# The second branch's gate as seven half-size block products per pair of tiles, in a hybrid attention and mLSTM layer

## The chip, the cores and the metric
The kernel runs on one core of one Trainium2 chip. The metric is the device time of one execution, in microseconds; the time shown is the median of three runs. All of the layer's large products are done on TensorE (PE) in fp32 quality: each operand x is split into a high part h (rounded to the matmul format) and a low part l = x - h, and a product is three matmuls, h·h, l·h and h·l. A split is one ScalarE (ACT) copy and one VectorE (DVE) subtraction. SyncE (SP) and GpSimd (POOL) issue most of the DMAs.

## The reference
One layer of a decoder on 512 tokens of width 1024: a norm, one combined input projection, two mixers side by side (block-sparse attention and a chunked mLSTM), merged by two sigmoid gates, an output projection, and a SwiGLU FFN.
```
u = rms_norm(h, norm_mix_g)
qa, ka, va, qk_b, vb, ob, ib, fb, ga, gb = jnp.split(u @ w_in, IN_SPLITS, axis=-1)
ya = moba_attention(rope(qa), rope(ka), va)              # 512 wide
hb = mlstm_chunkwise(qb, kb_, vb, i_pre, f_pre)          # 4 heads x 128
hb = hb * lax.rsqrt(jnp.mean(hb * hb, axis=-1, keepdims=True) + NORM_EPS)
yb = jax.nn.sigmoid(ob) * (hb * mlstm_norm_g)
merged = jax.nn.sigmoid(ga) * (ya @ w_proj_a) + jax.nn.sigmoid(gb) * (yb @ w_proj_b)
h = h + merged @ w_out
h = h + swiglu(rms_norm(h, norm_ffn_g))
return rms_norm(h, norm_final_g)
```
The gates ga and gb are 1024 wide each. The change concerns gb, and the order of what stands around it.

## The kernel before, in words
Everything is kept transposed: a result tile has 128 output columns as partitions and the 512 tokens along the free axis. The input projection and the branch projections are cut into 52 units of 128 output columns (`UNITS`), taken in one fixed order: q, k, va, ob, vb, qkb, then the gates ga 0 to 7 (units 28 to 35) and gb 0 to 7 (36 to 43), then p 0 to 7 (44 to 51). A unit's weights are 128x1024 numbers. SP loads them into a `raw` buffer (seven of these), two units at a time (`load_pair`); `split_unit` (line 206) splits them into `wh` and `wl`, two units ahead of their use; `proj` runs 24 matmuls of 128x512 (`mm3`, lines 213 to 215), and `run_g` (line 592) takes the result from PSUM with one DVE multiplication by the norm's factor `rb`. A unit p holds w_proj_a and w_proj_b for 128 columns: 12 matmuls on ya, 12 on yb, then two sigmoids on ACT and three DVE steps that make a tile of the merged vector mT (lines 612 to 614).

Between the units, the mixers' own instructions are interleaved by a loop over steps (`n`): attention for 16 steps, the mLSTM for 8. Its norm runs per head in three parts: `ml_d1` (squares and a copy `nsb` of the numerator), `ml_d2` (the mean, then rsqrt as Ln, Exp and one Newton step, with lines 334 to 336 from a helper) and `ml_e` (the output gate, and the split of yb).

Behind the units comes `ffn()`. The output projection is done as seven block products (W11, W12, S1, S2, S4, S3, W22) on half the tokens and sums of weight blocks, in place of eight; the sums are formed in DRAM, by an SP copy and an accumulating POOL DMA (`wo_copy`, `wo_sum`), at the unit numbers that the table `SUMS` gives. Its operands (`bq`) are sums and differences of the halves of mT, split in turn (`quarters_a`, `quarters_b`, `quarters_lo`). The FFN's gate and up products follow, 22 items of seven products of 12 matmuls 128x256 each; three of them have their weight sums formed in DRAM too (`gs`, `gt24`).

The Tile scheduler sets each engine's order by priorities. The code's order gives them; inside `ffn()`, `plan` and `at` place work by assumed costs (5440 for a product of the output projection) plus the numbers in the table `Q`.

Of the kernel before, what the change touches and what calls it, by code (L numbers as in the profile page):

```python
# [88 lines left out]
Q = {'leadW11': 9908, 'leadW12': 4893, 'leadS1': 11032, 'leadS2': 5165, 'leadS4': 2571, 'leadS3': 5137, 'leadW22': 3430, 'step': -3359, 'hl': 7300, 'addW11': -1192, 'addW12': 2824, 'addS1': 2078, 'addS2': 1620, 'addS4': 7560, 'addS3': 14758, 'addW22': -1247, 'x': 1583, 'g11': 10592, 'g13': 20503, 'g24': 641, 'g12': 5084, 't00': 3558, 't10': -367, 't11': -569, 't01': 1348, 'sq': 641, 'ev': 300, 'qlo': 8915, 'q4': 4375, 'q35': -263, 'q5': -627, 'q26': -426, 'q6': 3684, 'n2': -7624, 'n2b': -1704, 'base': 294, 'mq': -9909, 'mqs': -14706, 'f35': 1, 'ld0': 6835, 'ld1': 20096, 'ld2': 16796, 'lw': 0, 'ho': 1622, 'lo': 2050, 'so': -829, 'nfirst': 5, 'ldS2': 4505, 'ldS4': 20963, 'ldS3': 22228, 'ldW22': 17677, 'mW12': 6692, 'mS2': 12719, 'mS4': 20328, 'mS3': 3928, 'mW22': 16520}  # L89
# [7 lines left out]
def hybrid_layer_kernel(ctx: ExitStack, tc, xT, xtm, wall, wwo, wgu, wds, wdl, g3v, vecs, wgates, consts, rope, out):  # L97
# [90 lines left out]
    wstate = {"pair": 0, "split": 0}  # L188
# [3 lines left out]
    def load_pair():  # L192
        p = wstate["pair"]
        if p * 2 >= NU:
            return
        for u in (2 * p, 2 * p + 1):
            raw[u] = blk(name="raw", raw=True)
            nc.sync.dma_start(raw[u], wall[u])
        wstate["pair"] += 1

    def split_unit():
# [176 lines left out]
    def fill(n=1, mid=None):  # L378

        for _ in range(n):  # L380
# [5 lines left out]
            while wstate["split"] <= min(u + LOOK, NGEN - 1):  # L386
# [195 lines left out]
    gz = {}  # L582

    def run_g(kind):
        def fn(i, wh, wl):
# [7 lines left out]
            gz[(kind, i)] = z  # L593
        return fn
# [7 lines left out]
    def run_p(m, wh, wl):  # L602
        if m % 4 == 0:
            mT.append(slot4(name="mT"))
        pa, pb = mmb(), mmb()
        mm3(pa, wh, wl, range(4), [t[0] for t in ya], [t[1] for t in ya], True, True)
        marks["p", m] = mm3(pb, wh, wl, range(4, 8), [t[0] for t in yb], [t[1] for t in yb], True, True)
        yield
        ga, gb = gz.pop(("ga", m)), gz.pop(("gb", m))
        act_(ga, ga, AF.Sigmoid)  # L610
        act_(gb, gb, AF.Sigmoid)
        V.tensor_tensor(ga, pa, ga, op=ALU.mult)
        V.tensor_tensor(gb, pb, gb, op=ALU.mult)
        V.tensor_tensor(mT[m // 4][:, m % 4, :], ga, gb, op=ALU.add)
# [102 lines left out]
    def wo_sum(k, src):  # L717
        if src == "g":
# [669 lines left out]
    def ffn():  # L1388
# [42 lines left out]
        fill(2)  # L1431
# [283 lines left out]
    def ml_c(h, b, ats):  # L1715
# [3 lines left out]
        for j in ((0, 1), (2, 3))[b]:  # L1719
# [6 lines left out]
            T.matmul(o, vh[:, v], al, start=False, stop=j == 3)  # L1726
# [6 lines left out]
    def ml_d1(h):  # L1733
# [4 lines left out]
        V.tensor_copy(nsb, num)  # L1738
# [3 lines left out]
    def ml_d2(h, sqn, d2, nsb):  # L1742
# [4 lines left out]
        V.scalar_tensor_tensor(d2, d2, EPS * 128.0, ps, op0=ALU.mult, op1=ALU.add)  # L1747

        V.tensor_scalar(d2, d2, 2.0**-39, None, op0=ALU.mult)
# [36 lines left out]
    while n < len(steps) or qa or qb:  # L1786
# [30 lines left out]
        while qb and (qb[0][4] <= n - LC):  # L1817
# [37 lines left out]
def _pack(inp):  # L1855
# [8 lines left out]
    qk = _tiles(w_in[:, np.concatenate(cols)])  # L1864
    parts = {
# [68 lines left out]
```

## Time and profile before
| | |
|---|---|
| median of 3 runs | 727.38 us (727.01 to 727.42) |
| the profiled execution | 727.58 us |
| its span (first to last instruction) | 725.7 us |
| mean granted TensorE clock | 0.997 |
| input products, gates among them, until | 303.0 us of the span |
| projection units p | 303.0 to 346.5 us |
| output projection, FFN, final norm | from 346.5 us |
| moved by DMA | 133.68 MB, 184 GB/s in the mean |

The profile is of one execution. Busy times are shares of the span; the page's chain follows the work that ended last backwards. Row groups give the source line, the engine, the operation, the tile names (written<-read), the shapes, the count, busy time and mean duration, and the idle time ahead with what ended it.

### The profile page before, as it was taken

What the parts mean: (1) busy time and instruction counts of PE and PEld (TensorE: products, weight loads), DVE (VectorE), ACT (ScalarE), POOL (GpSimd) and SP (SyncE); (2) the same over time, 40 slices, a digit from 0 to 9 for tenths busy, and PEclk for the clock granted to TensorE, in tenths of its full rate; (3) what the DMA queues carried; (4) which work ended last, traced back from release to release, by engine and by line L of the source; (5) the groups of instructions that cost most, each with busy time, mean ns of one, the idle gap of its engine ahead of it and who ended that gap; (6) DMA issues with size and microseconds to landing.
All of it is one profiled execution on the core that took longest, in us unless ns stands there. A gap on an engine that the chain in (4) does not pass through costs nothing.

```text
span 725.7 us, 11396 instructions
## 1 busy us (share of the span) xinstructions
PE 715.8 (99%) x4167; PEld 632.4 (87%) x4167; DVE 623.4 (86%) x1090; ACT 441.7 (61%) x778; POOL 78.7 (11%) x100
## 2 busy tenths in 40 slices
PE   8999999999999999999999999999999999999995
PEld 6888888888888888888889998999899899899984
DVE  6898886899986688578898998899899899989997
ACT  7534767679755347633678666565555665655555
POOL 0004010101020001000000001300310310220000
PEclk9999999999999999999999999999999999999998
DMA  9778563856576656644594654975985795696403
GB/s 313 279 219 224 186 210 103 224 225 168 202 177 157 172 146 146 219 145 149 136 293 120 203 161 119 239 208 148 206 256 132 175 275 162 155 249 199 153 0 117
DMA packets 54649, 133.68 MB, mean 184 GB/s; under 512 B 5676, under 2 KB 10420, under 8 KB 54464
## 3 DMA queue, kind: packets, MB, share of 16 engines
q1 hardware_dynamic: 38272, 97.73, 39.1%
q0 software_dynamic: 14880, 32.82, 24.8%
q10 hardware_dynamic: 1440, 2.39, 0.9%
q8 instruction: 33, 0.54, 0.3%
q14 instruction: 24, 0.20, 0.1%
HBM read 116.11 MB, written 29.66 MB: 201 GB/s over the span
## 4 chain that ended last, share of the span: by engine, by line
PE 98%; DMA 1%; ACT 0%; issue 0%; DVE 0%; SPq 0%; DVEq 0%; ACTq 0%
PE mm L213 11%; PE mm L215 11%; PE mm L214 11%; PE mm L904 6%; PE mm L905 6%; PE mm L906 6%; PE s L904 3%; PE s L906 3%; PE s L905 3%; PE mm L1155 3%; PE mm L1156 3%; PE mm L1157 3%; PE acc L1649 2%; PE mm L496 2%; PE mm L497 2%; PE mm L498 2%
## 5 line engine op out<-in xcount | busy, mean ns | idle before, releaser
L160 ACT ACTIVATE wh<-raw 128x1024 fp32r<-128x1024 f32 x50 | 52.8, 1058 | 62.5 <-PE mm L214 59.7
L904 PE MATMUL mm<-bq,w 128*128 128x256 f32 x264 | 75.3, 285 | 0.0
L905 PE MATMUL mm<-bq,w 128*128 128x256 f32 x264 | 75.1, 284 | 0.0
L906 PE MATMUL mm<-bq,w 128*128 128x256 f32 x264 | 74.9, 284 | 0.0
L160 ACT ACTIVATE w<-raw 128x1024 fp32r<-128x1024 f32 (+2 forms) x63 | 58.7, 944 | 23.5 <-PE mm L214 10.0
L173 DVE TENSOR_TENSOR wl<-raw,wh 128x1024 fp32r<-128x1024 f32 x50 | 60.6, 1219 | 7.6 <-ACT wh L160 6.8
L851 DVE TENSOR_TENSOR w<-s,w 128x1024 fp32r<-128x1024 f32 x42 | 51.2, 1218 | 7.1 <-ACT w L160 7.1
L213 PE MATMUL mm<-u,wh 128*128 128x512 f32 x136 | 53.6, 394 | 0.0
L215 PE MATMUL mm<-u,wh 128*128 128x512 f32 x136 | 53.2, 391 | 0.0
L214 PE MATMUL mm<-u,wl 128*128 128x512 f32 x136 | 53.2, 391 | 0.0
L213 PE MATMUL mm<-uh,wh 128*128 128x512 f32 x136 | 53.0, 390 | 0.0
L214 PE MATMUL mm<-uh,wl 128*128 128x512 f32 x136 | 53.0, 390 | 0.0
L215 PE MATMUL mm<-ul,wh 128*128 128x512 f32 x136 | 53.0, 390 | 0.0
L160 ACT ACTIVATE w<-s 128x1024 fp32r<-128x1024 f32 (+1 forms) x46 | 46.6, 1019 | 8.4 <-DVE s L861 4.1
L904 PEld LDWEIGHTS mm<-bq,w 128*128 128x128 f32 x264 | 50.7, 192 | 0.4 <-ACT s L160 0.3
L906 PEld LDWEIGHTS mm<-bq,w 128*128 128x128 f32 x264 | 50.7, 192 | 0.0
L905 PEld LDWEIGHTS mm<-bq,w 128*128 128x128 f32 x264 | 50.7, 192 | 0.0
L904 PE MATMUL s<-bq,w 128*128 128x256 f32 x176 | 50.0, 284 | 0.0
L906 PE MATMUL s<-bq,w 128*128 128x256 f32 x176 | 49.9, 284 | 0.0
L905 PE MATMUL s<-bq,w 128*128 128x256 f32 x176 | 49.9, 284 | 0.0
L777 POOL DMA_DIRECT2D s<-in_wgu_dram x19 | 16.7, 881 | 230.3 <-DVE s L1200 53.1
L160 ACT ACTIVATE s<-mm 128x256 f32<-128x256 f32 x44 | 16.6, 377 | 29.8 <-PE mm L906 29.8
(433 smaller groups left out, 2249.5 us busy)
## 6 DMA issues: line engine op xcount, KB each, us to landing
raw<-in_wall_dram SPq DMA_DIRECT2D x50, 512.0 KB, 4.6
raw<-in_wgu_dram SPq DMA_DIRECT2D x22, 512.0 KB, 5.3
raw<-in_wds_dram SPq DMA_DIRECT2D x20, 512.0 KB, 8.0
s<-in_wgu_dram SPq DMA_DIRECT2D x19, 512.0 KB, 5.5
s<-in_wgu_dram POOLq DMA_DIRECT2D x19, 512.0 KB, 6.1
w<-in_wgu_dram SPq DMA_DIRECT2D x22, 256.0 KB, 6.4
ws<-in_wwo_dram POOLq DMA_DIRECT2D x8, 512.0 KB, 8.2
raw<-ws SPq DMA_DIRECT2D x8, 512.0 KB, 3.6
```

The costliest lines, as they stand in the source:

```text
L160: return A.activation(out_, in_, func, **kw)
L173: V.tensor_tensor(l, src, f(h), op=ALU.subtract)
L213: T.matmul(ps, wh[:, c], rh[j], start=start and j == 0, stop=False)
L214: T.matmul(ps, wl[:, c], rh[j], start=False, stop=False)
L215: i = T.matmul(ps, wh[:, c], rl[j], start=False, stop=stop and j == n - 1)
L851: V.tensor_tensor(dst[1], src, f(dst[0]), op=ALU.subtract)
L904: T.matmul(ps, wh[:, c], bh, start=first and k == 0, stop=False, skip_group_check=not first)
L905: T.matmul(ps, wl[:, c], bh, start=False, stop=False, skip_group_check=not first)
L906: i = T.matmul(ps, wh[:, c], bl, start=False, stop=k == 3, skip_group_check=not first)
L1155: T.matmul(ps, bh, wh[:, d], start=first and k == 0, stop=False, skip_group_check=not first)
L1156: T.matmul(ps, bh, wl[:, d], start=False, stop=False, skip_group_check=not first)
L1157: T.matmul(ps, bl, wh[:, d], start=False, stop=k == 1, skip_group_check=not first)
```

## The change
The eight gb units become four pairs. For a pair of weight tiles, the 1024 weight rows are cut into two halves and the two tiles stand for two blocks of output columns; the token axis is cut into two halves (`A_`, `B_`). This makes a 2x2 by 2x2 block product, done with seven products on half the tokens instead of eight: W11, S2, S1, W12, S3, S4, W22, each 4 x 3 matmuls of 128x256 (`gt_prod`). The weight sums S1 to S4 of a pair are formed in DRAM (`p13`, `p24`) by an SP copy, an accumulating POOL DMA, a second copy and two more accumulating DMAs (`pair_sums`, at the unit numbers in `PS`). The products' token operands are sums of halves of u: x is loaded from DRAM again (`t_load`), scaled by the norm's weight on ACT (`t_scale`), and four operand tiles `top` are formed and split (`t_ops`). The results of a pair are collected by ACT copies and DVE additions (`gt_main`, `gt_last`). One of a pair's two tiles comes out negated, which its sigmoid undoes by a scale of -1.

The units p are divided in pa (two column tiles of w_proj_a per unit) and pb (the same of w_proj_b). PE's order is now ga 0 to 5, pa 0, pa 1, ga 6, ga 7, pa 2, the first pair's W11, pa 3, the rest of the pairs' products (the next pair's W11 stands ahead of a pair's last two products), pb 0 to 3. The sigmoid of ga follows its own product. In the mLSTM's norm, `nsb`'s copy and the Newton step's square move from DVE to ACT and the multiplication by 2^-39 is folded into other instructions; the rsqrt (`ml_d3`) and `ml_e` are called at steps of the pair stage. All values of `Q` are set anew, and the sums for the output projection and `gt24` are formed later.
```
+GATES = [("ga", 6), ("ga", 7)] + [("gb", m) for m in range(8)]
+GPAIRS = [(("gb", 2 * i), ("gb", 2 * i + 1)) for i in range(4)]
...
+PS = {
+    14: [(0, 0), (1, 0)], 17: [(0, 1)], 18: [(1, 1), (2, 0)], 19: [(0, 2)], 20: [(2, 1), (0, 3), (3, 0)], 21: [(1, 2)],
...
+    def t_ops():
+
+        (a, b), (a2, b2) = ((t[:, :, A_], t[:, :, B_]) for t in ux)
+
+        def cut(o, src):
+            t = slot4(F32R, "top").rearrange("p (x k) (e c) -> p x (k e) c", x=2, e=2)
+            top[o] = t
+            act_(t[:, 0], src, AF.Copy)
+            V.tensor_tensor(t[:, 1], src, f(t[:, 0]), op=ALU.subtract)
+
+        V.tensor_tensor(b2, b2, b, op=ALU.subtract)
+        V.tensor_tensor(b, a, b, op=ALU.subtract)
+        cut(1, b)
+        V.scalar_tensor_tensor(a, b2, -1.0, a, op0=ALU.mult, op1=ALU.subtract)
+        cut(4, a)
+        cut(5, b2)
+        V.scalar_tensor_tensor(a2, a, -1.0, a2, op0=ALU.mult, op1=ALU.subtract)
+        cut(6, a2)
...
+    def gt_prep(i):
+
+        g = gtw[i]
+        g["W11"] = split_hl(g["w11"], "w11")
+        for j, (a, b) in enumerate((("S1", "S3"), ("S2", "S4"), ("W22", "W12"))):
+            h, l = split_hl(g[j], dst=(blk2(F32R, "w"), blk2(F32R, "w")))
+            g[a], g[b] = (h[:, 0, :], l[:, 0, :]), (h[:, 1, :], l[:, 1, :])
+            load_pair(1)
+            yield
...
+    def gt_prod(ps, w, o, first=False):
+        wh, wl = w
+        for k in range(4):
+            c = slice(k * P, (k + 1) * P)
+            bh, bl = gt_op(o, k)
+            T.matmul(ps, wh[:, c], bh, start=first and k == 0, stop=False, skip_group_check=not first)
+            T.matmul(ps, wl[:, c], bh, start=False, stop=False, skip_group_check=not first)
+            i = T.matmul(ps, wh[:, c], bl, start=False, stop=k == 3, skip_group_check=not first)
+        marks["unit"] = raw_ins(i)
...
+    def gt_main(i):
+        g = gtw[i]
+        x, s, t, u = g["x"], g["s"], g["t"], g["u"]
+        gt_prod(x, g["S2"], 4)
+        act_(s[:, B_], x, AF.Copy)
         yield
+        z = g["z"] = sb()[:, A_]
+        gt_prod(z, g["S1"], 1, first=True)
+        act_(t[:, B_], z, AF.Copy)
+        yield
+        y = accb()[:, A_]
+        gt_prod(y, g["W12"], 2, first=True)
+        V.tensor_tensor(u[:, A_], y, s[:, A_], op=ALU.add)
+        yield
+        gt_prod(x, g["S3"], 5)
+        V.tensor_tensor(t[:, B_], x, t[:, B_], op=ALU.add)
+        yield
+
+    def gt_last(i):
+        g = gtw.pop(i)
+        x, z, s, t, u = g["x"], g["z"], g["s"], g["t"], g["u"]
+        gt_prod(z, g["S4"], 3)
+        V.tensor_tensor(u[:, B_], z, s[:, B_], op=ALU.add)
+        V.tensor_tensor(t[:, B_], t[:, B_], rb[:, B_], op=ALU.mult)
+        yield
+        gt_prod(x, g["W22"], 6)
+        V.tensor_tensor(t[:, A_], x, rb[:, A_], op=ALU.mult)
+        V.tensor_tensor(u, u, rb, op=ALU.mult)
+        gz[GPAIRS[i][0]], gz[GPAIRS[i][1]] = t, u
+        yield
...
+    def pair_sums(i, j):
+
+        c = lambda x: wgt[i][:, None, S * x : S * x + S].to_broadcast([P, 2, S])
+        if j == 0:
+            nc.sync.dma_start(p13[i], c(0))
+        elif j == 1:
+            nc.gpsimd.dma_start(p13[i], wgt[i][:, 512:1536].rearrange("p (x c) -> p x c", x=2), accum_op=ALU.add)
+        elif j == 2:
+            nc.sync.dma_start(p24[i], p13[i][:, 0:1, :].to_broadcast([P, 2, S]))
+        elif j == 3:
+            nc.gpsimd.dma_start(p24[i], c(2), accum_op=ALU.add)
+        else:
+            nc.gpsimd.dma_start(p24[i][:, 1, :], wgt[i][:, 1536:2048], accum_op=ALU.add)
...
-        V.tensor_copy(nsb, num)
+        act_(nsb, num, AF.Copy)
...
-        V.tensor_scalar(d2, d2, 2.0**-39, None, op0=ALU.mult)
...
-        t = newton(r, d2, lambda: slot(name="nt"))
+        act_(t, r, AF.Square)
+        V.scalar_tensor_tensor(t, t, -(2.0**-40), d2, op0=ALU.mult, op1=ALU.mult)
+        V.scalar_tensor_tensor(t, t, 1.5, r, op0=ALU.add, op1=ALU.mult)
...
+        if n in (24, 25):
+            t_load(n - 24)
+        if n in (24, 26):
+            with behind("unit" if n == 26 else "c"):
+                t_scale(n // 26)
...
+    late = {}
     for h in range(4):
-        if UNITS[pos[0]][0] != "p":
-            fill(1)
-        ml_e(h, norms_out[h])
-    while pos[0] < len(UNITS) and UNITS[pos[0]][0] != "p":
-        fill(1)
+        late.setdefault(Q["d%d" % h], []).append(lambda h=h: ml_t.__setitem__(h, ml_d3(h)))
+    for h in range(4):
+        late.setdefault(Q["e%d" % h], []).append(lambda h=h: ml_e(h))
+    gt_stage(late)
     ffn()
```
Three places of the new order follow; numbers behind names only tell buffers apart, and line numbers are those of each kernel.

DVE, where yb's last head is made ready and the last units begin. Before: `gb` is a gate's evacuation, `wl` the low part of a unit's weights, `yb` that of a head's output.
```order
L1763 SCALAR_TENSOR_TENSOR nt_2913<-nt_2913,vec,ob_2254 128x512
L592 TENSOR_TENSOR gb_3029<-mm_3003,rn_359 128x512
L173 TENSOR_TENSOR yb_3034<-nt_2913,yb_3034 128x512
L173 TENSOR_TENSOR wl_3074<-raw_2924,wh_3073 128x1024
L592 TENSOR_TENSOR gb_3066<-mm_3041,rn_359 128x512
L173 TENSOR_TENSOR wl_3109<-raw_2999,wh_3108 128x1024
```
After: `gg` and `gu` are a pair's two result tiles.
```order
L765 TENSOR_TENSOR gg_3394<-mm_3392,gg_3394 128x256
L772 TENSOR_TENSOR gu_3395<-s_3471,gs_3393 128x256
L187 TENSOR_TENSOR yb_3294<-nt_3143,yb_3294 128x512
L187 TENSOR_TENSOR yb_3356<-nt_3151,yb_3356 128x512
L773 TENSOR_TENSOR gg_3394<-gg_3394,rn_367 128x256
L2001 SCALAR_TENSOR_TENSOR nt_3211<-nt_3211,vec,ob_2276 128x512
L776 TENSOR_TENSOR gg_3394<-mm_3392,rn_367 128x256
L777 TENSOR_TENSOR gu_3395<-gu_3395,rn_367 128x512
L187 TENSOR_TENSOR yb_3356<-nt_3211,yb_3356 128x512
L187 TENSOR_TENSOR wl_3545<-raw_3390,wh_3544 128x1024
L664 TENSOR_TENSOR gg_2977<-mm_3549,gg_2977 128x512
```
Heads 1 and 2 of yb now stand behind pair 3's first evacuations, and the last head behind all of them, next to pb's splits; before, the last head stood ahead of the last two evacuations of gb.

SP, in the loads for the pairs. Before: `gt` is gt24, copied from the sum `gs`.
```order
L198 DMA raw_2999<-in_wall_dram 128x1024
L709 DMA gt_282<-gs_285 256x1x512
L198 DMA raw_3001<-in_wall_dram 128x1024
L198 DMA raw_3077<-in_wall_dram 128x1024
L198 DMA raw_3079<-in_wall_dram 128x1024
```
After: `p` are the sums in DRAM, `in_wgt` the pairs' weights, `in_wall` from the third row off pb's.
```order
L942 DMA gs_293<-in_wgu_dram 256x1x512
L715 DMA raw_3140<-p_286 128x1024
L715 DMA raw_3180<-p_290 128x1024
L939 DMA gt_282<-gs_293 256x1x512
L715 DMA raw_3270<-in_wgt_dram 128x2x512
L1004 DMA w_3920<-in_wgu_dram 128x512
L209 DMA raw_3290<-in_wall_dram 128x1024
L209 DMA raw_3319<-in_wall_dram 128x1024
```
The copy of gt24 stands between pair 3's sums and its W22/W12, ahead of all loads of pb.

PE, at the second product of the output projection. Before: W12 (`acc`, operand `bq_3457`) runs bank by bank.
```order
L914 MATMUL acc_3518<-w_3363,bq_3457 128x512
L915 MATMUL acc_3518<-w_3364,bq_3457 128x512
L916 MATMUL acc_3518<-w_3363,bq_3457 128x512
L914 MATMUL acc_3532<-w_3351,bq_3457 128x512
L915 MATMUL acc_3532<-w_3352,bq_3457 128x512
L916 MATMUL acc_3532<-w_3351,bq_3457 128x512
```
After: `mm` is W11, `s` is S1.
```order
L1149 MATMUL mm_3780<-w_3667,bq_3625 128x512
L1147 MATMUL acc_3806<-w_3671,bq_3745 128x512
L1148 MATMUL acc_3806<-w_3672,bq_3745 128x512
L1147 MATMUL acc_3820<-w_3671,bq_3745 128x512
L1148 MATMUL acc_3820<-w_3672,bq_3745 128x512
L1147 MATMUL s_3872<-w_3687,bq_3629 128x512
L1148 MATMUL s_3872<-w_3688,bq_3629 128x512
L1149 MATMUL s_3872<-w_3687,bq_3629 128x512
```
Two matmuls of W12 for each bank, which read the high part of operand 2 alone, now stand ahead of S1, and the rest of W12 behind it.

More of the change, by code (lines that the diff above doesn't have):

```diff
@@ L187, in hybrid_layer_kernel, with unit_load, load_pair @@
     whl = {}
-    wstate = {"pair": 0, "split": 0}
+    wstate = {"pair": 0, "split": 0, "end": NPLAIN + 2}
     NU = len(UNITS)
     LOOK = 2
[L192 to L199, printed above, removed]
+    gtw = {}
+    def unit_load(u):
+        raw[u] = blk(name="raw", raw=True)
+        nc.sync.dma_start(raw[u], wall[u])
+    jobs = [(unit_load, u) for u in range(2, NPLAIN)]
+    jobs += [(lambda j: gt_load(0, j), j) for j in range(3)]
+    jobs += [(unit_load, u) for u in (NPLAIN, NPLAIN + 1)]
+    jobs += [(lambda x: gt_load(*x), (i, j)) for i in range(1, len(GPAIRS)) for j in range(3)]
+    jobs += [(unit_load, u) for u in range(NPLAIN + 2, NU)]
+    def load_pair(n=2):
+        for _ in range(n):
+            if jobs:
+                job, x = jobs.pop(0)
+                job(x)
     def split_unit():
@@ new lines, in hybrid_layer_kernel, with t_load, t_scale @@
+    run["pb"] = run_pb
+    A_, B_ = slice(0, S // 2), slice(S // 2, S)
+    top = {}
+    ux = []
+    def t_load(j):
+        if True:
+            t = slot4(name="ux")
+            for k in range(4):
+                nc.sync.dma_start(t[:, k, :], xT[4 * j + k])
+            ux.append(t)
+    def t_scale(j):
+        t = ux[j]
+        for k in range(4):
+            act_(t[:, k, :], t[:, k, :], AF.Copy, scale=col(G1 + 4 * j + k))
+    def t_ops():
[13 more added lines that the diff above has]
+        cut(6, a2)
@@ new lines, in gt_stage, with seq @@
+    def gt_stage(extra):
+        n = len(GPAIRS)
+        step = 0
+        def seq():
+            for i in range(n):
+                if i == 0:
+                    fill(1)
+                    next(preps[0], None)
+                    gt_first(0)
+                    yield
+                    fill(1)
+                    next(preps[1])
+                yield from gt_main(i)
+                if i == 2:
+                    wstate["end"] = NGEN
+                    split_unit()
+                if i + 1 < n:
+                    gt_first(i + 1)
+                    next(preps[i + 1])
+                    yield
+                g = gt_last(i)
+                next(g)
+                if i + 1 < n:
+                    next(preps[i + 1])
+                if i == 2:
+                    split_unit()
+                yield
+                next(g)
+                if i + 2 < n:
+                    next(preps[i + 2])
+                extra.setdefault(Q["g%d" % i], []).extend([lambda k=k, c=c: logistic(k, c) for k, c in zip(GPAIRS[i], (-1.0, 1.0))])
+                yield
+        for _ in seq():
+            with behind("unit"):
+                for job, k, src in SUMS.get(("gt", step), ()):
+                    (wo_copy if job else wo_sum)(k, src)
+            for x in extra.pop(step, ()):
+                p_ = tc.cur_priority
+                tc.cur_priority = p_ + Q["low"]
+                x()
+                tc.cur_priority = p_
+            step += 1
+        for s in sorted(extra):
+            for x in extra[s]:
+                x()
@@ L1725, in ml_c @@
             T.matmul(o, vl[:, v], ah, start=False, stop=False)
-            T.matmul(o, vh[:, v], al, start=False, stop=j == 3)
+            marks["c"] = raw_ins(T.matmul(o, vh[:, v], al, start=False, stop=j == 3))
         if b == 1:
```

145 lines of the change are left out of this document (111 added, 34 removed), and 9 rows, old and new, of tables (PS, SUMS).

## The prediction
> **What bounds the kernel now.** I read the page first, for its share of busy time and its chain; of the page's parts 1 and 4 these lines carry it:
> ```profile
> span 725.7 us, 11396 instructions
> PE 715.8 (99%) x4167; PEld 632.4 (87%) x4167; DVE 623.4 (86%) x1090; ACT 441.7 (61%) x778; POOL 78.7 (11%) x100
> PE 98%; DMA 1%; ACT 0%; issue 0%; DVE 0%; SPq 0%; DVEq 0%; ACTq 0%
> ```
> PE is busy for 715.8 of 725.7 us and the chain that ended last is PE for 98%. A change in the middle therefore counts as PE time plus the holes that it opens in PE's row. Next I read the stages, as windows: the last part of the input products, five gate units alone, the eight projection units, a piece of the FFN of 120 matmuls 256 wide (ten products of twelve), the first three together, and the long stretch ahead of them. The columns are the window, its length, then busy time of PE, PEld, DVE, ACT, POOL, the granted clock, the DMA share and GB/s.
> ```profile
> 243.61:275.75 32.14, 32.14 (x148) 26.74 (x148) 22.81 (x34) 12.06 (x18) 2.42 (x3) 1.00 0.64 175
> 275.75:302.96 27.21, 27.21 (x121) 22.53 (x120) 21.43 (x30) 20.91 (x35) 1.85 (x2) 1.00 0.57 149
> 302.96:346.48 43.52, 43.52 (x193) 36.06 (x192) 32.76 (x42) 16.73 (x20) 0.00 (x0) 1.00 0.51 170
> 468.71:483.11 14.40, 14.40 (x123) 14.40 (x121) 14.25 (x24) 9.47 (x16) 0.00 (x0) 1.00 0.88 258
> 243.61:346.48 102.87, 102.87 (x460) 85.34 (x460) 77.00 (x105) 49.70 (x71) 4.27 (x5) 1.00 0.57 166
> 85.00:243.61 158.61, 158.60 (x822) 135.57 (x821) 132.16 (x303) 109.15 (x233) 13.56 (x18) 1.00 0.64 183
> ```
> In each row PE's busy time is the window: there is no hole to win back, at full clock. So the change can gain only by giving PE less to do. Two prices follow. 512 wide: 43.52 / 192 = 0.2267 us each (27.21 / 120 gives the same). 256 wide: 14.40 / 120 = 0.1200 us. Twice 0.1200 is 0.0133 more than 0.2267: a narrow matmul carries a fixed part of about 13 ns that halving doubles. DVE is the engine next to PE: 77.00 of 102.87 us here (25.9 idle), 14.25 of 14.40 in the FFN piece.
>
> **The change, part by part.**
>
> *PE.* Eight gate units of 24 matmuls, 512 wide, go: 192 x 0.2267 = 43.5 us. Four pairs of 7 x 12 matmuls, 256 wide, come: 336 x 0.1200 = 40.3 us. Net -3.2 us. The projection keeps its 192 matmuls in other units: nothing.
>
> Against the price taken stands a page. The Trainium skill, "TensorE: Matmul & The Clock Gate", section Back-to-back issue gap, gives an isolated spacing of N/2.4 + 2.5 ns, so 109 and 216 ns, by which the sum would be 36.7 - 41.4 = -4.7 us. The trace's 120 and 227 ns are both longer, and the measurement decides.
>
> *DVE.* Durations are these rows of the groups by form, the first seven from 243.6 to 346.5 us, the last from the FFN.
> ```profile
> L173 DVE TENSOR_TENSOR wl<-raw,wh 128x1024 fp32r<-128x1024 f32 x15 | 18.3, 1220 | 1.6 <-ACT wh L160 1.6
> L592 DVE TENSOR_TENSOR gb<-mm,rn 128x512 f32<-128x512 f32 x8 | 5.5, 688 | 10.1 <-PE mm L215 10.1
> L613 DVE TENSOR_TENSOR gb<-mm,gb 128x512 f32<-128x512 f32 x7 | 4.8, 690 | 6.9 <-PE mm L215 6.9
> L1738 DVE COPY nsb<-acc 128x512 f32<-128x512 f32 x3 | 2.1, 688 | 3.1 <-PE acc L1725 2.9 <-ACT sqn L160 0.2
> L1749 DVE TENSOR_SCALAR d<-d 128x512 f32<-128x512 f32 x4 | 1.6, 420 | 0.0
> L334 DVE TENSOR_TENSOR nt<-ri 128x512 f32<-128x512 f32 x4 | 2.8, 690 | 0.4 <-ACT ri L165 0.3
> L657 DVE TENSOR_TENSOR mT<-mT 128x1024 f32<-128x1024 f32 x1 | 1.2, 1215 | 0.0
> L1109 DVE SCALAR_TENSOR_TENSOR up<-s,s 128x256 f32<-128x256 f32 x19 | 7.9, 417 | 0.8 <-PE s L906 0.8
> ```
> Weight splits: each pair splits three tiles of 1024 and one of 512 columns, 12 x 1.22 + 4 x 0.69 = 17.4, less eight at 1.22: +7.6. The operand sums (t_ops): eight instructions of 1024 columns, +9.8. Evacuation: per pair five of 256 columns (0.417) and one of 512, 11.1, less eight at 0.69: +5.6. The mLSTM norm gives up per head the nsb copy (0.69), the 2^-39 multiplication (0.42) and newton's square (0.69): -7.2. Sum +15.8 us, so 92.8 busy in a stretch of 102.9 - 3.2 = 99.7 us; idle falls from 25.9 to 6.9 us. I count all of it in this stretch, which is the hard case, as part of the operand sums and of the earlier ya splits may fall ahead of it.
>
> *ACT.* From the same views:
> ```profile
> L160 ACT ACTIVATE wh<-raw 128x1024 fp32r<-128x1024 f32 x14 | 14.8, 1059 | 30.9 <-PE mm L214 30.2 <-PE mm L215 0.7
> L165 ACT ACTIVATE gb<-gb 128x512 f32<-128x512 f32 x8 | 4.9, 617 | 0.0
> L160 ACT ACTIVATE s<-mm 128x256 f32<-128x256 f32 x35 | 13.2, 377 | 27.7 <-PE mm L906 27.7
> L153 ACT ACT_TABLE_LOAD x2 | 2.6, 1283 | 0.0
> ```
> Weights 12 x 1.06 + 4 x 0.62 - 8 x 1.06 = +6.7; scaling the second copy of x, 8 x 0.62 = 4.9; high parts of the operands 4 x 1.06 = 4.2; product copies 12 x 0.377 = 4.5; nsb copy and square 8 x 0.62 = 5.0; two more table loads 2.6. Sum 27.9: 49.7 + 27.9 = 77.6 of 99.7 us, with 22 left. ACT doesn't become the bound; what it can do is be late for DVE in single places.
>
> *DMA.* A pair's sums are a chain in DRAM: copy, accumulate, copy, accumulate, accumulate. The nearest transfers, from the list of DMA issues:
> ```profile
> gs<-in_wgu_dram SPq DMA_DIRECT2D x3, 512.0 KB, 6.7
> gs<-in_wgu_dram POOLq DMA_DIRECT2D x3, 512.0 KB, 6.8
> gt<-gs SPq DMA_DIRECT2D x1, 512.0 KB, 5.3
> gt<-in_wgu_dram POOLq DMA_DIRECT2D x1, 512.0 KB, 7.6
> gt<-in_wgu_dram POOLq DMA_DIRECT2D x1, 256.0 KB, 5.1
> ```
> 6.7 + 6.8 + 5.3 + 7.6 + 5.1 = 31.5 us of landings per pair. The chains start with unit 14 and must end some 160 us later: hidden five times over, four chains running beside each other. The traffic grows by about 19 MB (estimate: 9 in those chains, 5 more as the accumulating ones read and write, 2 for x again, 3 as a pair loads 1.75 MB where two units loaded 1); at 183 GB/s for a share of 0.64 that adds about 0.25 over the 260 us from 85 to 346, to 0.9 at most. The FFN piece runs at 0.88 with PE full, so I cost this at nothing. If that cover failed, loads would be late for the splits, and PE with them.
>
> The copy of gt24 is now moved past raw loads of pair 3 on SP: it waits for a sum in DRAM, and the loads of W22/W12 of pair 3 and of the pb units stand behind it. Before, sum and copy ran so:
> ```profile
> 260.93 0.55 SPq L712 DMA_DIRECT2D gs<-in_wgu_dram  x1
> 265.72 0.81 POOL L725 DMA_DIRECT2D gs<-in_wgu_dram  x1 [17.59 <-DMA gs<-in_wgu_dram]
> 272.13 0.53 SPq L709 DMA_DIRECT2D gt<-gs  x1
> ```
> From first copy to second 11.2 us; by landings 13.5. I replayed the new order by hand, each engine's queue in turn with these durations: the loads behind the copy have some 18 us until their splits, so it costs nothing; it would if it took over 20.
>
> *Handovers.* DVE's low part waits for ACT's high part of the same tile, and PE for both. Where DVE is short of time, this is what is seen:
> ```profile
> 270.45 1.23 DVE L173 TENSOR_TENSOR wl<-raw,wh 128x1024 fp32r<-128x1024 f32 x1 [0.17 <-ACT wh L160]
> ```
> 0.17 us each. In my replay each pair's weights are ready 0.6 to 3 us ahead of their product, tightest pair 3's first three and yb's last head, ready 0.3 us before pb 0. New stalls are thus bounded by 0 (the FFN piece, where DVE is 99% busy and PE has no hole) and, in this mild form, 14 splits of the last two pairs and the pb units x 0.17 = 2.4. No reason gives a gain below nothing, as PE had no holes. I take 0.8, a third of the way up, nearer the FFN row since it is the same arrangement of seven products.
>
> *The step into the out-projection.* Before, the last mT and operand 2 follow the last projection matmul (346.48):
> ```profile
> 347.41 0.69 DVE L614 TENSOR_TENSOR mT<-ga,gb 128x512 f32<-128x512 f32 x1
> 349.29 1.23 DVE L648 TENSOR_TENSOR bq<-mT,bq 128x1024 fp32r<-128x1024 f32 x1
> ```
> Operand 2 is whole at 350.5, under W11's 5.44 us (24 x 0.2267). Now its low part follows eight DVE instructions, about 8.5 us behind mT; but PE's order puts S1 whole between the first rows of W12 and its rest, so W11 and S1 cover 10.9 us. Nothing.
>
> Sum: the profiled execution took 727.58 us for its span of 725.7; 727.58 - 3.2 + 0.8 = 725.2. It lies 0.2 above the median shown, 727.38, so I forecast 725.0.
>
> **The rivals.** A measurement of this kernel tells some 0.2% from no change, 1.45 us.
>
> *Handovers eat the gain.* 14 x 0.17 = 2.4 us of stalls: 727.4 - 3.2 + 2.4 = 726.6, within 0.2%. For it: leads of under 1 us at two places. Against: DVE's 6.9 us of idle, and the FFN row. 0.20.
>
> *DVE becomes the bound, and it is slower.* Place: from pair 2 to the first pb units, where the mLSTM norms, the pairs' evacuation and the splits meet. It decides when more than 6.9 us of DVE's idle time can't be filled. Before, 25.9 us are idle, 17.0 of them in the two rows of groups that wait for a PE product (10.1 and 6.9). If half of the 25.9 stays unusable (13.0), DVE ends 6.1 us late: 727.4 - 3.2 + 6.1 = 730.3. For it: an in-order queue with evacuations among the splits. Against: shorter products make shorter waits for evacuation. 0.12.
>
> *Narrow matmuls wait for their weights.* If PE could not hide a weight load behind 256 columns, the pair stage would go at the load's mean:
> ```profile
> L904 PEld LDWEIGHTS mm<-bq,w 128*128 128x128 f32 x264 | 50.7, 192 | 0.4 <-ACT s L160 0.3
> ```
> 336 x 0.192 = 64.5 instead of 43.5 us: 748. It decides above 43.5 / 336 = 0.1295 us per matmul. The same FFN loads are within 0.120 us from start to start, so they overlap, and it needs another cause to be slower here. The same section of the Trainium skill says that in a stream of loads and matmuls the spacing is set by both, 81 ns for 128 columns and 131 for 512; no row here is as short as 131 for 512. 0.03.
>
> *It doesn't do what it says* (the products don't become narrow or stay as many): 727.4. The new order of PE holds 336 rows 256 wide for the 192. 0.02.
>
> **How the numbers follow.** Forecast 0.63, faster by 2.4 us (0.33%). Same: 0.20 + 0.02 = 0.22. Slower: 0.12 + 0.03 = 0.15. The low end is the lowest run shown without a stall, 727.0 - 3.2 = 723.8, less 0.3 for the spread of runs: 723.5. The high end takes in the handovers (726.6) and the milder half of the DVE rival, up to 729.0; what is left out is the rest of it, the weight rival, and little below: under 0.2. All cases of the forecast's sign lie from 723.5 to 725.9.
>
> **What would show it.** In the windows: PE without holes from pair 0 to the last pb unit, 40.3 us of 256-wide matmuls at 0.120; DVE over 90% busy there, ACT under 80%. The prediction is wrong if PE or PEld shows waits for w or yb from DVE adding up to over 1.5 us, if gt24's copy holds SP until the W22 loads of pair 3 are late, if PE waits at the W12 product of the out-projection for operand 2, or if matmuls of the pair stage are not 0.120 apart.

## The result and the profile after

The changed kernel takes 737.30 us (median of 6 runs, 734.69 to 738.99) against 727.63 for the kernel before (6 runs, 727.01 to 728.37): ratio 1.0130, 95% interval 1.0119 to 1.0141. It is slower by 9.7 us where a gain of 2.4 was forecast, outside the range. Its runs spread over 4.3 us, those of before over 1.4. The profiled run took 735.35 us for a span of 733.6.

The page's parts 1 and 4 of the changed kernel, busy time by engine and the chain that ended last:
```profile
span 733.6 us, 11793 instructions
PE 717.1 (98%) x4311; PEld 637.6 (87%) x4311; DVE 636.5 (87%) x1110; ACT 467.0 (64%) x820; POOL 90.0 (12%) x112
...
PE 83%; DMA 6%; issue 5%; DVE 3%; ACT 2%; POOL 0%; SPq 0%; POOLq 0%; ACTq 0%; DVEq 0%
```
The chain is no longer PE alone: 17% of it are transfers, issues, DVE and ACT. DVE (+13.1 us) and ACT (+25.3) grew about as forecast (+15.8 and +27.9), so the sizes of the engines' work are not what failed.

The pairs' stage first, as windows of the changed kernel: 324 matmuls of the pairs with nothing between them, the same stretch on to the last pb unit, then the out-projection behind it.
```profile
292.29:331.90 39.61, 39.30 (x324) 38.92 (x323) 33.89 (x53) 31.78 (x52) 2.68 (x3) 1.00 0.90 266
292.29:353.63 61.34, 61.03 (x420) 56.80 (x419) 55.37 (x83) 45.11 (x69) 2.68 (x3) 1.00 0.76 227
353.63:430.00 76.37, 76.37 (x484) 68.74 (x483) 73.86 (x118) 57.31 (x105) 5.31 (x6) 1.00 0.68 205
```
324 narrow matmuls take 39.30 us, 0.1213 each (0.1200 was used), with one hole of 0.31; the out-projection has none. So neither is where the 9.7 us went. PE's waits say where. The columns are the total, the count, and the longest:
```profile
PE s L1932 <- DVE R L1935: 3.8, 1, 3.8
PE s L1791 <- DMA ks<-sd: 1.0, 1, 1.0
PE mm L242 <- DVE ga L625: 0.7, 1, 0.7
PE mm L738 <- ACT gs L174: 0.3, 1, 0.3
```
The 3.8 us lie some 85 us ahead of the first pair, in the mLSTM. R is the broadcast of a head's gates to all partitions, 896 KB, which POOL issues for each head shortly before use. The rows around the hole, from the timelines of PE, DVE, POOL and SP:
```profile
205.43 0.39 PE L1932 MATMUL s<-qk 128*128 128x256 f32 x1 [3.79 <-DVE R L1935]
199.59 1.14 DVE L1913 SCALAR_TENSOR_TENSOR R<-con,cS,R 128x128 f32<-128x128 f32 x4 [3.49 <-DMA R<-scr]
187.59 0.80 POOL L1901 DMA_DIRECT2D R<-scr  x1 [10.23 <-PE s L1934]
188.37 2.17 POOL L930 DMA_DIRECT2D p<-in_wgt_dram  x2
186.81 1.13 SPq L945 DMA_DIRECT2D ws<-ws  x2
187.99 1.23 SPq L945 DMA_DIRECT2D ws<-in_wwo_dram  x2
```
R is issued at 187.6 and lands at 199.6. Beside it stand four copies of 512 KB (`ws`, sums for the output projection) and two accumulating transfers of pair sums (`p`). DVE stands idle for 3.5 us at R, with the rest of its queue behind, and PE waits for DVE. R itself is issued 3.0 us later than in the kernel before, as POOL waits for PE, and PE had already lost time at other waits, the keys (`ks`) among them. In the kernel before, the same broadcast had the queues nearly to itself:
```profile
184.55 0.58 POOL L1668 DMA_DIRECT2D R<-scr  x1 [12.59 <-PE s L1701]
195.65 1.11 SPq L715 DMA_DIRECT2D ws<-ws  x2
```
Its landing, from the view of that tile in this stretch, before and then after:
```profile
DMA to landing us min/median/max: 4.8/4.8/4.8
```
```profile
DMA to landing us min/median/max: 12.0/12.0/12.0
```
What a hole does to PE beyond its own length stands in three windows of the changed kernel, ahead of the hole, in it, and a little behind it (the third column from the end is the granted clock):
```profile
197.00:201.40 4.40, 4.40 (x23) 3.69 (x21) 1.81 (x6) 1.42 (x3) 0.00 (x0) 1.00 1.04 271
201.40:205.40 4.00, 0.24 (x2) 0.04 (x1) 4.00 (x7) 3.95 (x8) 0.00 (x0) 1.00 1.11 255
206.76:210.17 3.41, 3.41 (x10) 2.63 (x9) 2.24 (x5) 3.38 (x6) 0.00 (x0) 0.50 0.11 43
```
PE is idle for 3.8 us, and then runs 3.41 us at half the clock, which costs another 1.7 (an estimate: half of 3.41). The whole stage was slowed in its transfers, from the lists of DMA issues, before and after:
```profile
ws<-in_wwo_dram POOLq DMA_DIRECT2D x8, 512.0 KB, 8.2
R<-scr POOLq DMA_DIRECT2D x4, 896.0 KB, 5.0
```
```profile
p<-in_wgt_dram POOLq DMA_DIRECT2D x8, 512.0 KB, 12.7
ws<-in_wwo_dram POOLq DMA_DIRECT2D x8, 512.0 KB, 11.0
R<-scr POOLq DMA_DIRECT2D x4, 896.0 KB, 8.4
```

### The profile page after: what moved, and what is told of

Same layout as the page of the kernel before. It is cut to its first block, busy times and chain, and to the rows that moved or that the text cites. A ratio compares the mean times of both kernels' runs of the same rounds, so it can differ in the third digit from the quotient of the medians.

```text
span 733.6 us, 11793 instructions
## 1 busy us (share of the span) xinstructions
PE 717.1 (98%) x4311; PEld 637.6 (87%) x4311; DVE 636.5 (87%) x1110; ACT 467.0 (64%) x820; POOL 90.0 (12%) x112
## 2 busy tenths in 40 slices
DMA packets 61883, 148.39 MB, mean 202 GB/s; under 512 B 6252, under 2 KB 10996, under 8 KB 61696
## 4 chain that ended last, share of the span: by engine, by line
PE 83%; DMA 6%; issue 5%; DVE 3%; ACT 2%; POOL 0%; SPq 0%; POOLq 0%; ACTq 0%; DVEq 0%
PE mm L242 6%; PE mm L243 6%; PE mm L244 6%; PE mm L1137 6%; PE mm L1138 6%; PE mm L1139 6%; DMA R<-scr 4%; PE s L1137 3%; PE s L1139 3%; PE s L1138 3%; PE mm L1388 2%; PE mm L1389 2%; PE mm L1390 2%; PE acc L1138 1%; PE acc L1137 1%
## 5 line engine op out<-in xcount | busy, mean ns | idle before, releaser
L174 ACT ACTIVATE w<-raw 128x1024 fp32r<-128x1024 f32 (+2 forms) x75 | 71.5, 962 | 22.0 <-PE mm L243 10.1
L174 ACT ACTIVATE wh<-raw 128x1024 fp32r<-128x1024 f32 x42 | 44.3, 1057 | 26.1 <-PE mm L243 21.2
L187 DVE TENSOR_TENSOR wl<-raw,wh 128x1024 fp32r<-128x1024 f32 x42 | 51.0, 1220 | 9.7 <-ACT wh L174 8.8
L242 PE MATMUL mm<-u,wh 128*128 128x512 f32 x104 | 41.7, 401 | 0.7 <-DVE ga L625 0.7
L244 PE MATMUL mm<-u,wh 128*128 128x512 f32 x104 | 41.3, 397 | 0.0
L243 PE MATMUL mm<-u,wl 128*128 128x512 f32 x104 | 41.2, 396 | 0.0
L242 PE MATMUL mm<-uh,wh 128*128 128x512 f32 x104 | 40.5, 389 | 0.0
L244 PE MATMUL mm<-ul,wh 128*128 128x512 f32 x104 | 40.5, 389 | 0.0
L243 PE MATMUL mm<-uh,wl 128*128 128x512 f32 x104 | 40.5, 389 | 0.0
## 6 DMA issues: line engine op xcount, KB each, us to landing
p<-in_wgt_dram POOLq DMA_DIRECT2D x8, 512.0 KB, 12.7
```

What stands on the lines that cost most here:

```text
L174: return A.activation(out_, in_, func, **kw)
L187: V.tensor_tensor(l, src, f(h), op=ALU.subtract)
L242: T.matmul(ps, wh[:, c], rh[j], start=start and j == 0, stop=False)
L243: T.matmul(ps, wl[:, c], rh[j], start=False, stop=False)
L244: i = T.matmul(ps, wh[:, c], rl[j], start=False, stop=stop and j == n - 1)
```

## The experiments

Theory A: transfers that the change adds or moves fall beside R's broadcasts and other transfers that are issued just ahead of their use; they land late, an in-order engine stands at them, and PE runs dry. Theory B: the holes come from what DVE and ACT now do in the mLSTM's last steps. Waits and landings are each from the one profiled run of a kernel, the times from all its runs. The times, with the ratio to the runs of the kernel before on the same chip:

| kernel | us, median (lowest to highest) | ratio, 95% interval |
|---|---|---|
| after | 737.30 (734.69 to 738.99) | 1.0119 to 1.0141 |
| no pair sums | 729.15 (728.55 to 730.57) | 1.0016 to 1.0037 |
| before, with pair sums | 730.84 (729.91 to 731.43) | 1.0034 to 1.0067 |
| pair sums as plain copies | 734.51 (733.48 to 735.92) | 1.0084 to 1.0115 |
| sums later | 728.83 (727.38 to 734.27) | 1.0007 to 1.0045 |
| sums later, x scaled later | 729.20 (728.66 to 730.13) | 1.0016 to 1.0035 |
| sums between, x scaled later | 729.50 (728.26 to 731.33) | 1.0020 to 1.0039 |
| no pair sums, `ws` at old times | 726.72 (726.57 to 727.60) | 0.9983 to 1.0002 |
| before, `ws` at new times | 730.47 (729.48 to 730.79) | 1.0024 to 1.0054 |
| sums between, evacuation first | 725.70 (725.41 to 727.59) | 0.9967 to 0.9985 |
| no pair sums, old times, evacuation first | 725.42 (725.12 to 726.09) | 0.9964 to 0.9985 |
| after, `ws` at old times | 728.23 (727.34 to 730.19) | 1.0004 to 1.0023 |
| before, evacuation first | 726.92 (726.60 to 727.41) | 0.9985 to 1.0003 |

The kernel before had medians of 727.28 to 727.38 in these sessions.

**No pair sums.**
```
-for u_, js in PS.items():
-    SUMS.setdefault(u_, []).extend((1 - j % 2 if j < 4 else 0, i, j) for i, j in js)
...
-        nc.sync.dma_start(n, (p13[i], p24[i], wgt[i].rearrange("p (x c) -> p x c", x=4)[:, 1:4:2])[j])
+        nc.sync.dma_start(n, (wgt[i][:, 0:1024].rearrange("p (x c) -> p x c", x=2), wgt[i][:, 1024:2048].rearrange("p (x c) -> p x c", x=2), wgt[i].rearrange("p (x c) -> p x c", x=4)[:, 1:4:2])[j])
```


> The changed kernel without the twenty DMAs that form the pairs' weight sums in DRAM: S1 to S4 are loaded straight from the weights, in the same sizes, so the second gate's values are not the reference's. Everything else stays. Theory A (traffic): the sums' transfers slow down the transfers for which the mLSTM and the attention wait; without them the broadcast R lands in about 5 us as before, PE has no hole near 201 us, its clock stays whole, and the time is 727.5 - 3.2 plus at most 1 of stalls: 724.3 to 725.5. Theory B (order and engine work): the holes come from what DVE and ACT now do in the mLSTM's last steps (sigmoids, table loads, the earlier splits of ya); the hole of about 4 us and the halved clock stay, and the time is 732 or more.

Measured 729.15: 8.2 us of the loss go, the hole near 201 us and the halved clock with them, so B does not hold for most of it. But it is 3.7 us above A's range. R's third broadcast explains why; without any pair sums it still landed in
```profile
DMA to landing us min/median/max: 10.0/10.0/10.0
```
The copies of `ws` at 186.8 to 189.2 in the rows above are not pair sums: the change had moved the output projection's sums there from another time. (A dozen rows of DVE and ACT also change places in this kernel, since the scheduler orders by when it thinks a transfer lands. Rows also change places in other versions that issue transfers at other times: in the kernel before with `ws` at new times, some of the DVE steps on R stand elsewhere. These versions therefore price transfers and order together; only the plain copies below keep every engine's order.)

**Before, with pair sums.**
```
+PS = {
+    14: [(0, 0), (1, 0)], 17: [(0, 1)], 18: [(1, 1), (2, 0)], 19: [(0, 2)], 20: [(2, 1), (0, 3), (3, 0)], 21: [(1, 2)],
...
+for u_, js in PS.items():
+    SUMS.setdefault(u_, []).extend((1 - j % 2 if j < 4 else 0, i, j) for i, j in js)
```


> The kernel before, with the changed kernel's twenty DMAs of pair sums added at the same unit numbers, on tiles in DRAM that nobody reads (same sizes, same kinds, same queues). Theory A (traffic): R lands in 7 us or more where it took 5, PE gets holes between 100 and 235 us, and the time rises by 3 to 9 us, to 731 to 737. Theory B (order and engine work): within 0.7 us of the kernel before.

Measured 730.84, 3.5 us more, just under A's range and far from B's, from transfers that nobody reads. R's third broadcast landed in 8.0 us, and PE's longest new wait is the attention's keys, another transfer issued just ahead of use:
```profile
PE s L1588 <- DMA ks<-sd: 1.5, 1, 1.5
```

**Pair sums as plain copies.**
```
-            nc.gpsimd.dma_start(p24[i], c(2), accum_op=ALU.add)
+            nc.gpsimd.dma_start(p24[i], c(2))
```
(and the same for the other two accumulating transfers of a pair)

> The changed kernel with the accumulation taken off the pair sums: the same twenty DMAs, same sizes and queues and the same order on every engine, but POOL's are plain copies; the second gate's values are not the reference's. Theory A in the form that bytes matter: an accumulating DMA moves its destination too, so about 5 of 14 MB go, the holes shrink by about a third, 731 to 735. Theory A in the form that accumulating is what is slow: 725 to 727. Theory B: as the changed kernel, 735 to 739.

Measured 734.51, in the range forecast for bytes: of the 8.2 us that the pair sums cost, 2.8 go, a third. But the page counts 148.39 MB moved in both kernels, so the 5 MB that accumulating was thought to add don't show in it. What does show is that POOL's 512 KB transfers of the sums land in 7.3 us in place of 12.7 (medians). With the same order on every engine, the run also shows that transfers alone move the time, by these 2.8 us. R's third landing took 10.9 us, and PE's hole was 2.7 us:
```profile
PE s L1932 <- DVE R L1935: 2.7, 1, 2.7
```

**Sums later.**
```
 SUMS = {
-    20: [(1, "S1", (1, 0))], 22: [(0, "S1", (1, 1))], 25: [(1, "S2", "S1"), (1, "S3", (0, 0))],
+    18: [(1, "S1", (1, 0))], 20: [(0, "S1", (1, 1))], 22: [(1, "S2", "S1"), (1, "S3", (0, 0))],
...
 PS = {
+    19: [(0, 0)], 21: [(0, 1)], 23: [(0, 2)], 25: [(0, 3)], 26: [(0, 4)],
+    28: [(1, 0)], 29: [(1, 1)], 30: [(1, 2)], 31: [(1, 3), (2, 0)], 32: [(1, 4)], 33: [(2, 1), (3, 0)],
+    34: [(2, 2), (3, 1)], 35: [(2, 3), (3, 2)], 36: [(2, 4), (3, 3)], 37: [(3, 4)],
```


> The changed kernel with the pair sums spread out: one chain after the other, from unit 19 to unit 37, most of it behind the mLSTM's last broadcast, and the output projection's sums back at the unit numbers that they had before. Theory A (traffic): fewer transfers beside the mLSTM's broadcasts, so most of the holes go: 725 to 730, the rest lost to late weights of pairs 2 and 3 where the sums end shortly before they are loaded. Theory B: 735 to 739, as the changed kernel.

Measured 728.83, in the range of A, but from 727.38 to 734.27. Its profiled run is the slowest (734.27), and the hole has moved to another transfer. The timelines of ACT and PE:
```profile
261.28 1.37 ACT L174 ACTIVATE ux<-ux,vec 128x512 f32<-128x512 f32 x2 [6.11 <-DMA ux<-in_xT_dram]
262.56 0.62 ACT L174 ACTIVATE sqh<-sqn 128x512 fp32r<-128x512 f32 x1
```
```profile
272.51 0.79 PE L1977 MATMUL s<-sqh,onesr 128*128 128x512 f32 x1 [4.68 <-ACT sqh L174]
```
ACT stands 6.1 us at the scaling of the second copy of x, whose load lands late beside the sums of pairs 2 and 3; the squares of the last head stand behind it, and PE waits 4.7 us. From 271.65 us, 0.9 before PE resumes, its clock is at half for 6.82 us:
```profile
271.65:278.47 6.82, 5.96 (x14) 4.70 (x15) 6.81 (x9) 3.22 (x5) 0.62 (x1) 0.50 0.88 181
```

**Sums later, x scaled later.**
```
-        if n in (24, 26):
-            with behind("unit" if n == 26 else "c"):
-                t_scale(n // 26)
+        if n == 24:
+            with behind("c"):
+                t_scale(0)
         if n == 27:
+            with behind("unit"):
+                t_scale(1)
```


> The kernel with the sums later, with one step moved: the scaling of the second half of the second copy of x on ACT is placed one step later, behind the last head's squares. Theory A (a late transfer blocks an in-order engine): in the version with the sums later ACT stood 6.1 us at this scaling, waiting for x, with the squares' split queued behind it and PE 4.7 us idle waiting for that; now ACT gets past, the hole and the halved clock behind it go, and the time is 724.5 to 726.5 with little spread. Rival: PE's hole comes from the squares themselves or from weights that land late; then it stays, at 728 to 734.

Measured 729.20. The hole at the squares and the large spread are gone, as A says (728.66 to 730.13), but the time is a miss: the operand sums now come later on DVE, and a gate's evacuation behind them holds up a pair's W11:
```profile
PE mm L738 <- DVE ga L625: 1.8, 1, 1.8
```

**Sums between, x scaled later.**
```
+    19: [(0, 0)], 20: [(1, 0)], 21: [(0, 1), (1, 1)], 23: [(0, 2)], 25: [(0, 3), (1, 2)], 26: [(0, 4), (1, 3)],
+    28: [(2, 0)], 29: [(1, 4), (2, 1)], 31: [(2, 2)], 33: [(2, 3), (3, 0)],
+    34: [(2, 4), (3, 1)], 35: [(3, 2)], 36: [(3, 3)], 37: [(3, 4)],
```


> As the one before, with the pair sums placed between the broadcasts: the first step of pairs 0 and 1 ahead of R's first broadcast, every accumulation right behind one of the broadcasts, pairs 2 and 3 behind the last. Theory A (traffic beside the broadcasts, and late x): R lands in 4.5 to 6.5 us each time, x is earlier since less is moved at 225 to 265 us, and the time is 724.3 to 726.0. Rival (any added traffic costs, wherever it stands): 727 to 731.

Measured 729.50, in the rival's range. The profile shows the same 1.8 us of PE at the gate's evacuation and no other new hole over 0.5, so the hole taken over from the version above is at least part of the miss, and the run doesn't judge the placing by itself. (The version below that beats the kernel before keeps the placing, but changes two other things with it.)

**No pair sums, `ws` at old times.** The edit of "no pair sums", with the `SUMS` of "sums later", which are those of the kernel before for these transfers.

> The changed kernel without the pair sums (S1 to S4 loaded straight from the weights, so the second gate's values are not the reference's), and with the output projection's sums at the unit numbers that they had before. Theory A: without pair sums there was still a hole, as R's third broadcast landed in 10 us beside the output projection's copies, which the change had moved there; with these back it lands in 5 us and the time is 724.3 to 725.7, the forecast of the products alone. Rival (the rest of the loss is from DVE, ACT or the pair stage): 728.5 to 730.

Measured 726.72: 2.4 us less than with `ws` at the new times, where the edit differs only in the units at which sixteen transfers are issued. R's third broadcast lands in 4.3 us. It is still 1.0 above A's range; the hole left is at R's fourth broadcast, and again DVE's queue stands at a late transfer, with a gate's evacuation behind:
```profile
221.26 1.14 DVE L1911 SCALAR_TENSOR_TENSOR R<-con,cS,R 128x128 f32<-128x128 f32 x4 [3.37 <-DMA R<-scr]
222.32 0.68 DVE L623 TENSOR_TENSOR ga<-mm,rn 128x512 f32<-128x512 f32 x1
```
```profile
PE mm L240 <- DVE ga L623: 1.2, 1, 1.2
```

**Before, `ws` at new times.**
```
-    18: [(1, "S1", (1, 0))], 20: [(0, "S1", (1, 1))], 22: [(1, "S2", "S1"), (1, "S3", (0, 0))],
-    24: [(0, "S2", (0, 0))], 27: [(1, "S4", "S2")], 29: [(0, "S4", (0, 1))], 31: [(0, "S3", (1, 0))],
+    20: [(1, "S1", (1, 0))], 22: [(0, "S1", (1, 1))], 25: [(1, "S2", "S1"), (1, "S3", (0, 0))],
+    33: [(0, "S2", (0, 0)), (1, 0, None), (1, 1, None)], 35: [(0, "S3", (1, 0)), (1, "S4", "S2"), (0, 0, None)],
+    36: [(0, "S4", (0, 1)), (0, 1, None), (1, 2, None)], 37: [(0, 2, None)],
```


> The kernel before, with only the output projection's sums moved to the unit numbers of the changed kernel. Theory A: the copies fall on R's third broadcast, which lands in 8 us or more where it took 4.75; before's mixers had more room there, so the price is 0.3 to 2.5 us: 727.7 to 730. Rival: nothing, 727.4 within 0.3.

Measured 730.47, 3.2 us more, above A's range: a third of the whole loss from moving sixteen transfers that the kernel had all along. R's third broadcast, from the same view:
```profile
DMA to landing us min/median/max: 10.2/10.2/10.2
```
No wait of PE at this place is longer than 0.5 us, so the list of waits hides the price; the timelines show it. The same matmul behind R's product, in the kernel before and then here, where PE was still 0.3 us ahead at 198 us:
```profile
206.78 0.40 PE L213 MATMUL mm<-u,wh 128*128 128x512 f32 x1
208.56 0.50 PE L213 MATMUL mm<-u,wh 128*128 128x512 f32 x1
```
PE loses 2.1 us there, in several short gaps; by the profiled executions the whole price is 1.9 (729.48 against 727.58).

**Sums between, evacuation first**, the full computation: sums as in "sums between", x scaled where the change has it, and
```
         ml_load(h)
         yield
+        for _ in range(4 * (h == 3)):
+            yield
...
+        with behind(*["ev"] * (h == 3)):
+            for j in range(4):
+                w = r[KR[j][0]][:, KR[j][1]]
...
-                V.tensor_tensor(z, ps, rb, op=ALU.mult)
+                marks["ev"] = raw_ins(V.tensor_tensor(z, ps, rb, op=ALU.mult))
```


> The full computation: the pair sums between the broadcasts and the output projection's sums at their old unit numbers, x's scaling back at its place in the change, and the DVE steps that wait for R's last broadcast behind one more gate evacuation. Theory A: what is left of the loss are single late transfers in front of in-order queues; of the holes that the two versions before showed (2.0 us behind the operand sums, 4.7 at x, up to 1.3 at a gate's evacuation) none stays above 0.6 us, and the time is 725.0 to 726.8. Rival (the sums' traffic takes its price anywhere): 727.5 to 730.

Measured 725.70, in A's range, 1.6 us below the kernel before (0.9967 to 0.9985) and 11.6 below the changed kernel, with the same products and the same sums. The largest waits of PE from 85 us on, in a profiled run that is the slowest of its eleven (727.59; the others took 725.41 to 725.88):
```profile
PE s L1980 <- ACT sqh L174: 0.5, 1, 0.5
PE s L738 <- ACT gg L174: 0.4, 1, 0.4
PE mm L739 <- DVE w L187: 0.4, 1, 0.4
PE mm L738 <- ACT gs L174: 0.3, 1, 0.3
```

**No pair sums, old times, evacuation first.** "No pair sums, `ws` at old times" with that same edit.

> As the version without pair sums and with the output projection's sums at their old times, with the DVE steps that wait for R's last broadcast behind one more gate evacuation (the second gate's values are not the reference's). Theory A: the hole of 1.3 us there was the evacuation standing behind R's late landing; it goes to under 0.3 and the time falls from 726.7 to 725.2 to 725.9. Rival (R's steps are needed at once, so the wait moves to PE's product with R): 726.4 to 727.2.

Measured 725.42. The wait of 1.2 us is gone. The pair sums, well placed, thus cost 0.3 us (725.70 against 725.42), within what the runs can tell.

**After, `ws` at old times.** The changed kernel with the `SUMS` of "sums later" and its own `PS`.

> The changed kernel with only one step undone: the output projection's sums back at the unit numbers that they had before; the pair sums stay where the change put them. Theory A, with prices that add: moving those sums cost 2.4 us between the two versions without pair sums and 3.2 in the kernel before, so 737.3 falls to 733.5 to 735.5. Rival (both sets of sums press on the same broadcasts, and either alone is enough): R's third broadcast still lands in 9 us or more beside the pair sums, and the time stays at 736 to 739.

Measured 728.23, far below A's range: prices do not add. Undoing this one step takes back 9.1 of 9.7 us. The pair sums still make R's first two broadcasts land in 11.4 us at worst, but PE has no hole there; the third lands in
```profile
DMA to landing us min/median/max: 7.5/7.5/7.5
```
and PE's longest wait from 85 us on is 1.5 us, at the product with the keys.

**Before, evacuation first.**

> The kernel before with only the DVE steps that wait for R's last broadcast put behind one more gate evacuation: the control for the version that beat it. If that version's gain is from the half-size products, this stays at 727.0 to 727.4, as the hole there was only 0.3 us. If the gain was this edit, it falls to 725.7 to 726.5.

Measured 726.92, no difference that the runs can tell (0.9985 to 1.0003), a little under the first forecast and above the second. So this edit doesn't account for most of the gain of the version that beat both: 1.2 of 1.6 us are left for the products together with the new order around them. The two were not separated.

## Why the prediction was wrong

- **The products: right, a little dear.** Half-size products cost 0.1213 us per matmul in place of 0.1200 in the changed kernel, so the term of -3.2 us is nearer -2.8. The kernel without sums that has no late transfer left comes to 725.42, 1.9 under the runs of the kernel before beside it, where 2.4 was forecast for all of the change; it holds the moved DVE steps too. The rival of narrow matmuls waiting for weights did not occur.
- **Handovers: within the allowance.** 0.8 us were allowed from pair 0 to pb; the waits of the changed kernel show one of 0.3.
- **DVE as the bound: did not occur.** From pair 0 to the last pb unit DVE was busy for 90% (55.37 of 61.34 us), ACT for 74%, as forecast (over 90% and under 80%), and PE had 0.31 us of holes.
- **The copy of gt24 on SP and the step into the out-projection: right.** SP stood 3.6 us at the copy, waiting for the sum, well within the 18 us allowed, and PE waited neither for the loads behind it nor at W12.
- **The sums' transfers: wrong, and this is the step that failed.** The prediction took the share of the 16 DMA engines in a stage where everything is loaded ahead ("The FFN piece runs at 0.88 with PE full, so I cost this at nothing") as the price for a stage where it is not. The share itself came out as forecast (0.9 at most; 0.88 from 85 to 180 us), and the page's bytes grew by 14.7 MB (133.68 to 148.39) of the 19 estimated. What failed is "nothing": transfers that others wait for landed late all the same, R's third broadcast in 12.0 us in place of 4.8. With the pair sums taken out, 8.2 us of the loss go. What the runs point to is which transfer is issued just ahead of its use, and what is in flight beside it. The failed cover was named as late loads of weights; late were R and the keys, and x in a version with other times. None of the rivals held such a case.
- **The moved sums of the output projection: not priced at all.** The table `SUMS` was in the diff, but the sum has no term for it. Alone it costs 3.2 us in the kernel before, and undoing it alone takes back 9.1 us in the changed one.

The two steps cost more together than the sum of their prices. With `ws` at its old or new time, the kernel without pair sums takes 726.72 or 729.15 (+2.4), with them 728.23 or 737.30 (+9.1). R's third broadcast lands in 4.3, 10.0, 7.5 and 12.0 us in these four. At 7.5 us PE has no hole at R's product, as it has other work queued. At 10.0 and 10.2 us (the two kernels with `ws` at new times and no pair sums) the longest waits there are 0.5 and 0.4 us, with shorter gaps that bring it to 2.1 in the second. At 10.9 us (plain copies) the hole is 2.7 us and at 12.0 it is 3.8, each with 3.41 us at half the clock behind it. So the last 2 us of landing cost most. R's issue 2.8 us later (187.6 against 184.8 without pair sums) is a cost of its own: waits ahead of it, 1.0 at the keys and two of 0.5 and 0.4, had already held PE.

What stays open: why the runs of one kernel spread over 4 us. One piece of 3.41 us at half clock lowers the mean clock by 0.0023 and costs 1.7 us (estimates from 3.41 of some 730 us). The changed kernel's clock is 0.990 to 0.995 over its runs, that of before about 0.997, so between one and three such pieces a run would fit. The ten runs of the version with the sums between and x scaled later fall into two groups in the same way: 728.26 to 729.16 us at 0.997, 729.85 to 731.33 at 0.995. But only one run of each kernel was profiled, so this is not shown. Whether bytes or the accumulating itself make a part of the pair sums' price is open too: 2.8 of 8.2 us went with it (four runs), and the page counts the same bytes; sizes and numbers of transfers were not varied by themselves.

## What to carry to other kernels

A transfer that is "hidden five times over" for its reader can still be the dearest of the change, by what it delays: list the transfers that are issued shortly before their use, and price an added or moved one by what is in flight beside those, not by the mean share. When a table of times moves, price its moves as edits of their own. A change that looks wrong as a whole may need little more than its transfers re-timed: 737.3 became 725.7 that way, with one group of DVE steps moved as well.

## What the runs showed of the hardware

- In these profiles the clock halves around a long hole, for pieces of 3.41 us. Holes of 2.7 us (plain copies) and 3.8 us were each followed by one piece at 0.50, the one of 4.7 us by two (6.82 us at 0.50), the one of 1.8 us by none in its profiled run. In the 3.41 us ahead of the piece PE was busy for 1.06 us with the hole of 2.7 and for 1.33 with that of 3.8. Windows behind the hole of plain copies, and over that of the version with x scaled later (which ends at full clock):
```profile
204.02:207.43 3.41, 3.41 (x10) 2.64 (x9) 2.24 (x5) 3.38 (x5) 0.00 (x0) 0.50 0.05 17
```
```profile
278.00:281.90 3.90, 2.08 (x14) 1.68 (x15) 3.90 (x6) 2.92 (x3) 0.82 (x1) 1.00 1.01 330
```
  The Trainium skill, "TensorE: Matmul & The Clock Gate", section What's actually happening, has the halved clock follow an idle window of about 3.4 us that runs freely; the length of the pieces agrees, but here 2.7 us of idleness were enough.
- A broadcast of 896 KB that lands in 4.8 us with little beside it took 10.0 beside four 512 KB copies from another queue and 12.0 beside those and two accumulating transfers of its own queue behind it (loads of weights ran near it in all three). The Trainium skill, "DMA: Bandwidth & Descriptors", section Queues, rings and completion order, says that each DMA engine takes turns between the queues it has work for; the trace agrees in so far as R, issued first on its own queue, was slowed by what another queue held.
